# A scan over a matrix product: w loaded by row set over all partitions, other first cuts of x, and a shorter float32 warm-up of TensorE

## The chip, the cores and the metric

The kernel runs on one core of one Trainium2 chip. The metric is the device time of one execution in microseconds; the table below gives the runs. The engines are TensorE (PE, with its weight loads PEld), VectorE (DVE), ScalarE (ACT), GpSimd (POOL) and SyncE (SP); transfers are issued by SP, ACT and POOL and done by 16 DMA engines.

## The reference

```python
def setup_inputs():
    B, S, D = (16, 2048, 1024)
    return {'x': np.random.randn(B, S, D).astype(np.float32),
            'w': np.random.randn(D, D).astype(np.float32),
            'decay': (0.9 * np.random.rand(D) + 0.05).astype(np.float32)}

def reference(x, w, decay):
    xw = x @ w
    out[:, 0, :] = xw[:, 0, :].copy()
    for t in range(1, S):
        out[:, t, :] = decay[None, :] * out[:, t - 1, :] + xw[:, t, :]
```

A product of 32,768 rows with a 1024 x 1024 matrix, and then along the time axis of each batch a decayed running sum, with one decay for each column.

## The kernel before, in words

**Tiles.** The 16 x 2048 time steps are cut into 64 chunks of 512 (`TL`); two neighbouring chunks make a group. A group's product is made in eight slots of 128 output columns (`n`), each from eight sets of 128 rows of w (`k`): 4,096 products of 128 x 128 with 128 x 512 in bfloat16. The result stands with columns on partitions and time along the free axis, so VectorE can scan along time (`tensor_tensor_scan`, L229 and L210), transposes it back in 32 x 32 blocks (L266) into the `ot` buffers, and SP stores it.

**x.** A chunk is loaded by POOL in four DMAs, one for each quarter `q` of the 1024 columns of x; quarter `q` lands on partitions 32q to 32q+31, cast from float32 to bfloat16 on the way (`load`, L105). VectorE transposes 32 x 32 blocks of pairs of bfloat16 numbers, seen as float32 (`turn`, L115), into `xw`, in which the numbers of even and odd rows of w alternate; ScalarE or VectorE copies them apart into `xt` (`part`, L123). Some products read `xw` directly (`pairs`). Row `2p+e` of set `m` in quarter `q` of w thus meets partition `32q+p`.

**w.** w comes in four pieces `(h, e)`: half `h` of the columns, `e` for even or odd rows. A piece has four sets `m`. `load_w` (L307) loads a piece in four DMAs, one for each quarter of the partitions; each brings all four sets for its 32 partitions. Piece (0, 0) comes in float32, two DMAs from SP and two from ACT; the other three come from POOL, cast to bfloat16 (`load_part`, deeds U0 to U2). `settle` (L314) copies one set of a piece to `wsb`, in the order of columns that the products want (deeds W on VectorE, w on ScalarE). The staging buffers are the `ot` buffers of the output, not yet in use.

**The opening.** The first two chunks are handled in two parts each, whose sizes stand in `cuts`, in blocks of 32 time steps: 9 and 7 of chunk 0, 8 and 8 of chunk 1. For each part: load (deeds M0 to M3), transposition by set (E), copy by set (G on ScalarE, F on VectorE). The products of the first four slots go part by part: first part of chunk 0, all even sets and then all odd sets, four slots each; its second part in the same way; then chunk 1's first part by pairs of sets, and its second part slot by slot.

**Warm-up.** Before any data is there, TensorE multiplies zeros (`spin`, L332): 22 products of the zeroed tile `idle`, 128 x 512 in bfloat16. Then come `gate` products: for each quarter of x's first part, ScalarE copies one number of it into a zeroed tile `gate` (`spin_on`, L348, deeds K0 to K3), and TensorE makes products with that tile, 3, 3, 3 and 1 of them; so they start when that quarter has landed.

**Order.** The order of each engine's instructions is written out by hand: `agenda` lists deeds by slot, -99 is the opening, and every instruction is kept in program order on its engine (`pin`). The POOL queue has eight semaphores for its DMAs in turn: the ninth load waits at its issue for the landing of the first, and so on. The deed L takes the next x load of the list `loads`.

Of the kernel before, what the change touches and what calls it, by code (L numbers as in the profile page):

```python
# [9 lines left out]
FP32 = mybir.dt.float32  # L10
BF16 = mybir.dt.bfloat16
# [3 lines left out]
def _ap(ap_obj: bass.AP, new_ap, extra_offset=0):  # L15
    return dataclasses.replace(
        ap_obj,
        ap=[list(p) for p in new_ap],
        offset=ap_obj.offset + extra_offset,
    )  # L20
# [5 lines left out]
def kernel(  # L26
# [26 lines left out]
    nc = tc.nc  # L53
    pin = tc.keep_in_program_order
    B, S, D = x.shape
    assert w.shape == (D, D)

    NQ = 4
    P = 32
    CQ = D // NQ  # L60
    K = CQ // P
    M = K // 2
    TL = 512
    NJ = TL // P
    NC = S // TL
    R = K // 2
    CH = D // 2
    CR = CH // NQ

    const = ctx.enter_context(tc.tile_pool(name="const", bufs=1))  # L70
# [5 lines left out]
    def ring(pool, name, count, shape, dtype=FP32):  # L76
        i = turns[name] = turns.get(name, -1) + 1
        return pool.tile(shape, dtype, name=f"{name}{i % count}")

    def quad(q):  # L80
        return slice(q * P, (q + 1) * P)
# [12 lines left out]
    def ot_tile(nj):  # L94
        return ring(sb, "ot", 4, [128, nj, CR])
# [3 lines left out]
    xt_of = {}  # L99
# [25 lines left out]
    def matmul(ps, n, k, xt, t0=0, t1=TL, start=0, pairs=None):  # L125
        if pairs is None:
            rhs = xt[:, k // 2, k % 2, t0:t1]
        else:
            rhs = pairs[:, k // 2, t0 // P:t1 // P, :, k % 2].rearrange("p j i -> p (j i)")
        lhs = wsb[:, k, n].rearrange("p q i -> p (q i)")  # L130
        pin(nc.tensor.matmul(  # L131
            out=ps[:, t0:t1] if ps.shape[1] >= t1 else ps,
            lhsT=lhs,
            rhs=rhs,
            start=(k == 0 and t0 == start),
            stop=(k == K - 1),
        ))
# [3 lines left out]
    class Tile:  # L141
# [45 lines left out]
        def copy(self):  # L187
            self.xs = sb.tile([128, 2 * TL], FP32, name=f"xs{self.lot % 3}")[:, 0:self.T]
            size = self.T // len(self.parts())
            for i, ps in enumerate(self.parts()):  # L190
                pin(nc.scalar.copy(out=self.xs[:, i * size:(i + 1) * size], in_=ps))  # L191
# [82 lines left out]
    class Outlet:  # L274
# [8 lines left out]
        def store(self, b, t0):  # L283
# [4 lines left out]
            for j in range(0, self.nj, nj):  # L288
# [8 lines left out]

    room = [ot_tile(2 * NJ).rearrange("p j c -> p (j c)") for _ in range(2)]
    size = M * CH
    stage = {(0, 0): room[0][:, 0:size],  # L300
             (0, 1): room[0][:, size:size * 3 // 2].bitcast(BF16),
             (1, 0): room[1][:, 0:size // 2].bitcast(BF16),
             (1, 1): room[1][:, size // 2:size].bitcast(BF16)}

    def load_w(queues, h, e):
        for i, q in enumerate((0, 2, 1, 3)):
            pin(queues[i % len(queues)].dma_start(  # L307
                out=stage[h, e][quad(q)].rearrange("p (m d) -> p m d", m=M),
                in_=_ap(w, [[2 * D, P], [2 * P * D, M], [1, CH]],
                        (q * CQ + e) * D + h * CH)))  # L310

    def settle(h, e, m, copy):
        src = stage[h, e][:, m * CH:(m + 1) * CH]
        pin(copy(out=wcols[:, 2 * m + e, h],  # L314
                 in_=src.rearrange("p (q r i) -> p q r i", q=NQ, r=R)))

    idle = const.tile([128, TL], BF16, name="idle")
    spare = ring(psp, "spare", 1, [128, TL])
    rows = const.tile([128, 2, P], FP32, name="rows")
    touch = const.tile([128, 1], BF16, name="touch")  # L320
    load_w((nc.sync, nc.scalar), 0, 0)
    pin(nc.vector.memset(idle, 0.0))  # L322
    pin(nc.vector.memset(rows, 0.0))
    pin(nc.scalar.copy(out=touch, in_=idle[:, 0:1]))

    gates = [const.tile([128, 128], BF16, name=f"gate{q}") for q in range(NQ)]
    for gate in gates:
        pin(nc.vector.memset(gate, 0.0))

    def spin(count, by):  # L330
        for _ in range(count):
            pin(nc.tensor.matmul(out=spare, lhsT=by, rhs=idle, start=True, stop=True))  # L332

    spin(22, idle[:, 0:128])
    H = NJ // 2
    cuts = (((0, H + 1), (H + 1, NJ)), ((0, H), (H, NJ)))
    for q in range(NQ):
        pin(nc.sync.dma_start(
            out=rows[q * P:q * P + R],
            in_=_ap(decay, [[P, R], [CH, 2], [1, P]], q * CR)))  # L340
# [5 lines left out]

    def spin_on(q):
        pin(nc.scalar.copy(out=gates[q][quad(q), 0:1], in_=xb_of[0][quad(q), 0, 0:1]))  # L348
        spin(3 if q < NQ - 1 else 1, gates[q])

    def load_part(i):
        load_w((nc.gpsimd,), *((0, 1), (1, 0), (1, 1))[i])

    def part_one(i, copy):
        part(i // 8, copy, i % 4, i % 4 + 1, *cuts[i // 8][i // 4 % 2])
# [65 lines left out]
    def turn_and_load(c):  # L421
# [38 lines left out]
        "L": lambda i: load(*loads.pop(0)) if loads else None,  # L460
    }
    agenda = {
        -99: "M0 U0 M1 M2 M3 U1 U2 w0 W1 w2 W3 K0 K1 K2 K3 E0 E1 G0 E2 G1 E3 F2 G3 W4 w5 W6 W7 D E4 E5 G4 E6 G5 E7 F6 G7 E8 E9 G8 E10 G9 E11 F10 G11 E12 L E13 G12 L E14 G13 E15 L F14 G15",
        0: "p0 z0 W8 W9 W10 W11",
        1: "g0",
        2: "L S1 L",
# [89 lines left out]
    for step, (g, n) in enumerate(slots):  # L556
        T = TL * len(g)
        left = step - len(slots)
        if n % R == 0:
            ns, nj = range(n, n + R), T // P  # L560
            if left == -2 * R:
                outlets = [Outlet(ns, H, half) for half in range(2)]
            else:
                pieces = 1 if left < -7 * R else 2 if left < -6 * R else nj // H
                outlets = [Outlet(ns, nj, pieces=pieces)]
        if left == -R:
            outlets = []
        if step == 0:
            heads = [ring(psp, "ps", 3, [128, T]) for _ in range(3)]
            firsts = [ps[:, 0:TL] for ps in heads] + [spares[0]]  # L570
            seconds = [ps[:, TL:T] for ps in heads] + [spares[1]]
            for j0, j1 in cuts[0]:
                for e in range(2):
                    for k in range(e, K, 2):
                        for i in range(R):
                            matmul(firsts[i], i, k, xt_of[0], j0 * P, j1 * P, j0 * P,
                                   pairs=None if e else xw_of[0])
            for k0 in range(0, K, 2):
                for i in range(R):
                    for k in (k0, k0 + 1):  # L580
                        matmul(seconds[i], i, k, xt_of[1], 0, H * P,
                               pairs=xw_of[1] if k0 < 4 else None)
            for i in range(R):
                for k in range(K):
                    matmul(seconds[i], i, k, xt_of[1], H * P, TL, H * P,
                           pairs=xw_of[1] if i < 2 else None)
        if step < R:
            ps = heads[n] if n < 3 else tuple(spares)
        else:
            if step == K + 1:  # L590
                ps = nexts
            elif len(g) == 2 or n % R < 3:
                ps = ring(psp, "ps", 3, [128, T])
            else:
                ps = ring(psp, "spare", 1, [128, TL])
            todo = [(k, l) for k in range(K) for l in range(len(g))]
            if step < K:
                todo.sort(key=lambda kl: kl[0] % 2)
            elif step == K:
                todo = []  # L600
                nexts = (ring(psp, "spare", 1, [128, TL]), ring(psp, "ps", 3, [128, T])[:, TL:T])
                for l in range(len(g)):
                    for i, one in enumerate((ps[:, l * TL:(l + 1) * TL], nexts[l])):
                        for k in range(K):
                            matmul(one, n + i, k, xt_of.get(g[l]),
                                   pairs=xw_of[g[l]] if l or not i and k >= M else None)
            elif step == K + 1:
                todo = []
            if left == -1:
                ps = tuple(both[:, t:t + TL // 2] for t, both in zip(  # L610
                    (0, TL // 2), (ps, ring(psp, "ps", 3, [128, TL]))))
                blocks += [bank("spare1", 1), bank("ps", 3)]
                for t, half in zip((0, TL // 2), ps):
                    for k in range(K):
                        matmul(half, n, k, xt_of[g[0]], t, t + TL // 2, t)
                    if not t:
                        cross((1,), (0, 1))
                todo = []
            for k, l in todo:
                matmul(ps[:, l * TL:(l + 1) * TL], n, k, xt_of[g[l]])  # L620
        tiles.append(Tile(g, n, ps, outlets))
        do = agenda.get(step, agenda.get(left) if left >= -20 else None)
        if do is None:
            do = usual(step)
        else:
            do = do.split()
            if left == -20:
                do = rest(step) + do
        perform(do)
# [29 lines left out]
```

## Time and profile before

| what | value |
|---|---|
| median of 3 runs | 904.37 us (904.36 to 904.57) |
| profiled execution, its own time | 905.1 us |
| its span | 903.3 us |
| TensorE busy | 896.9 us (99%) |
| VectorE, ScalarE, GpSimd busy | 824.2, 685.9, 657.1 us |
| DMA moved | 204.77 MB, mean 227 GB/s |
| granted TensorE clock, mean | 1.000 |

The profile is of one execution; its times count from the start of the span. A row of the timeline gives start, duration, engine, line, operation, written tile <- read tiles, shapes and count, and in brackets how long the engine had been idle and what ended that. Stretches ("windows") give the busy time of each engine within them, then the granted clock, the DMA engines' share and GB/s. A load by POOL with a cast is counted with the bytes that it writes. A DMA's semaphore is raised in steps as its shares land; the trace holds the time of each step, and a landing is the last of them.

### The profile page before, as it was taken

Reading aid. Unit: us, or ns where it says so; the run is one execution under the profiler, and the core shown is the slowest. Engines: PE = TensorE matmul, PEld = TensorE weight load, DVE = VectorE, ACT = ScalarE, POOL = GpSimd, SP = SyncE. Lnnn points to the kernel's source line nnn. Section 1 sums busy time; section 2 is a strip of 40 time slices with the busy share of each in tenths; the row PEclk is TensorE's granted clock in tenths of the full one; section 3 lists DMA queues with packets and bytes.
Section 4 is the critical chain, followed back from the end, with each engine's and each line's share of the span. In section 5 each row is a group of like instructions: output and inputs, shape, how many; then the busy total and the mean of one; then the engine's idle time right before and its main releaser. Section 6 shows DMA issues by size and latency. Waiting matters only on the chain.

```text
span 903.3 us, 12163 instructions
## 1 busy us (share of the span) xinstructions
PE 896.9 (99%) x4216; PEld 412.8 (46%) x4216; DVE 824.2 (91%) x632; ACT 685.9 (76%) x957; POOL 657.1 (73%) x755
## 2 busy tenths in 40 slices
PE   9999999999999999999999999999999999999998
PEld 5444444444444444444444444444444444444444
DVE  4899998998999999999998999999999999999998
ACT  4899867877877877878778778777787787787743
POOL 7978678877767778777677687777777776876632
PEclk9999999999999999999999999999999999999999
DMA  9999999999999999999999999999999999999858
GB/s 193 184 215 215 223 244 208 215 229 232 248 239 251 253 241 246 250 258 249 241 237 226 222 231 226 232 229 227 233 227 226 233 231 222 227 230 214 184 143 232
DMA packets 403182, 204.77 MB, mean 227 GB/s; under 512 B 9392, under 2 KB 402096, under 8 KB 403120
## 3 DMA queue, kind: packets, MB, share of 16 engines
q1 hardware_dynamic: 265808, 134.77, 60.9%
q0 software_dynamic: 137024, 68.70, 56.4%
q8 instruction: 33, 0.54, 0.2%
q10 hardware_dynamic: 288, 0.52, 0.2%
q14 instruction: 29, 0.24, 0.1%
HBM read 138.42 MB, written 134.22 MB: 302 GB/s over the span
## 4 chain that ended last, share of the span: by engine, by line
PE 92%; DMA 3%; DVE 2%; issue 1%; POOL 1%; ACT 0%; DVEq 0%; POOLq 0%; ACTq 0%
PE ps L131 91%; DMA xb<-in_x_dram 2%; POOL xb L105 1%; DMA ot<-in_w_dram 1%; PE spare L131 1%; DVE so L229 1%; DVE ot L266 0%; DVE so L210 0%; DVE xw L115 0%; POOL xs L205 0%; PE spare L392 0%; PE ps L392 0%; ACT h L171 0%; DVE h L401 0%; POOL so L199 0%
## 5 line engine op out<-in xcount | busy, mean ns | idle before, releaser
L131 PE MATMUL ps<-xt,wsb 128*128 128x512 bf16 (+1 forms) x4024 | 865.6, 378 | 0.4 <-DVE so L229 0.4
L131 PEld LDWEIGHTS <-wsb 128*128 128x128 bf16 x4168 | 407.3, 98 | 479.0 <-issue 1.7
L205 POOL TENSOR_TENSOR xs<-h,xs 128x512 f32<-128x512 f32 (+1 forms) x190 | 242.8, 1278 | 183.1 <-ACT h L171 84.6
L266 DVE STREAM_TRANSPOSE ot<-so 128x1024 f32<-128x1024 f32 (+2 forms) x264 | 300.1, 1175 | 5.7 <-DMA out_dram<-ot 3.6
L191 ACT COPY xs<-ps 128x1024 f32<-128x1024 f32 (+1 forms) x190 | 188.8, 994 | 145.2 <-PE ps L131 141.6
L254 POOL TENSOR_TENSOR so<-h,xs 128x512 f32<-128x512 f32 (+1 forms) x190 | 241.1, 1271 | 48.0 <-ACT h L171 28.1
L123 ACT COPY xt<-xw 128x2048 bf16<-128x2048 bf16 (+3 forms) x136 | 242.1, 1788 | 8.9 <-DVE xw L115 8.9
L105 POOL DMA_DIRECT2D xb<-in_x_dram x264 | 174.2, 661 | 6.7 <-DMA xb<-in_x_dram 3.1
L171 ACT ACTIVATE h<-so,dec 128x512 f32<-128x512 f32 (+1 forms) x190 | 145.3, 765 | 37.3 <-DVE so L210 34.0
L115 DVE STREAM_TRANSPOSE xw<-xb 128x2048 f32<-128x2048 f32 (+3 forms) x78 | 147.4, 1902 | 8.8 <-DMA xb<-in_x_dram 8.8
L210 DVE TENSOR_TENSOR_SCAN so<-spare,keep,xs 128x512 f32<-128x512 f32 (+1 forms) x97 | 119.6, 1236 | 24.1 <-POOL xs L205 23.9
L210 DVE TENSOR_TENSOR_SCAN so<-spare,xs 128x512 f32<-128x512 f32 x93 | 113.2, 1219 | 26.4 <-POOL xs L205 23.5
L171 ACT ACTIVATE h<-ps,dec 128x512 f32<-128x512 f32 (+1 forms) x190 | 129.9, 683 | 0.0
L229 DVE TENSOR_TENSOR_SCAN so<-dec,ps 128x1024 f32<-128x1024 f32 x34 | 76.8, 2261 | 1.0 <-ACT h L171 1.0
L229 DVE TENSOR_TENSOR_SCAN so<-dec,keep,ps 128x1024 f32<-128x1024 f32 (+1 forms) x35 | 75.9, 2169 | 0.0
L258 ACT COPY keep<-so 128x1 f32<-128x1 f32 x136 | 25.3, 189 | 9.6 <-DVE so L229 9.0
L201 ACT COPY so<-keep 128x1 f32<-128x1 f32 x97 | 18.4, 191 | 2.7 <-DVE ot L266 2.5
L131 PE MATMUL ps<-xw,wsb 128*128 128x256 bf16 (+3 forms) x72 | 12.3, 306 | 0.4 <-DVE xw L115 0.4
L131 PE MATMUL spare<-xt,wsb 128*128 128x512 bf16 (+3 forms) x60 | 12.6, 330 | 0.0
L199 POOL MEMSET so<- 128x1 f32 x93 | 10.6, 116 | 0.6 <-DVE ot L266 0.6
L332 PE MATMUL spare<-idle 128*128 128x512 bf16 x22 | 7.4, 515 | 1.2 <-DVE idle L322 1.2
L307 POOL DMA_DIRECT2D ot<-in_w_dram x12 | 6.5, 545 | 1.0 <-issue 0.4
(39 smaller groups left out, 37.9 us busy)
## 6 DMA issues: line engine op xcount, KB each, us to landing
out_dram<-ot SPq DMA_DIRECT2D x236, 512.0 KB, 11.1
xb<-in_x_dram POOLq DMA_DIRECT2D x248, 256.0 KB, 7.9
out_dram<-ot SPq DMA_DIRECT2D x56, 128.0 KB, 2.6
out_dram<-ot SPq DMA_DIRECT2D x8, 256.0 KB, 4.0
ot<-in_w_dram POOLq DMA_DIRECT2D x12, 128.0 KB, 6.1
xb<-in_x_dram POOLq DMA_DIRECT2D x8, 128.0 KB, 4.8
out_dram<-xb SPq DMA_DIRECT2D x3, 256.0 KB
xb<-in_x_dram POOLq DMA_DIRECT2D x4, 144.0 KB, 6.2
```

The lines of the kernel that those rows point to most:

```text
L105: pin(nc.gpsimd.dma_start(out=xb_of[c][quad(q), j0:j1], in_=_ap(x, [[D, P], [P * D, j1 - j0], [1, CQ]], (b * S + t0 + j0 * P) * D + q * CQ)))
L115: pin(nc.vector.transpose(out=dst.rearrange("p (m j i) -> p j m i", m=M, i=P)[:, j0:j1, m0:m1], in_=src.rearrange("p (j m c) -> p j m c", ...
L123: pin(copy(out=xt_of[c][:, m0:m1, :, j0 * P:j1 * P], in_=src))
L131: pin(nc.tensor.matmul(out=ps[:, t0:t1] if ps.shape[1] >= t1 else ps, lhsT=lhs, rhs=rhs, start=(k == 0 and t0 == start), stop=(k == K - 1),))
L171: pin(nc.scalar.activation(out=h[:, i * size:(i + 1) * size], in_=src, func=mybir.ActivationFunctionType.Copy, scale=dec[:, self.n:self.n ...
L191: pin(nc.scalar.copy(out=self.xs[:, i * size:(i + 1) * size], in_=ps))
L205: pin(nc.gpsimd.tensor_tensor(out=odds, in0=self.g, in1=odds, op=ALU.add))
L210: pin(nc.vector.tensor_tensor_scan(out=so[:, 3:T + 2:2], data0=squares[-1][:, n:n + 1].to_broadcast([128, T // 2]), data1=self.xs[:, 1:T:2 ...
L229: pin(nc.vector.tensor_tensor_scan(out=so[:, t + 2:t + 2 + size], data0=dec[:, n:n + 1].to_broadcast([128, size]), data1=ps, initial=befor ...
L254: pin(nc.gpsimd.tensor_tensor(out=self.so[:, 2:T + 2:2], in0=self.h, in1=self.xs[:, 0:T:2], op=ALU.add))
L258: pin(nc.scalar.copy(out=self.keep, in_=self.so[:, self.T + 1:self.T + 2]))
L266: pin(nc.vector.transpose(out=outlet.ot[:, :, c0:c0 + P], in_=self.so[:, 2 + t0:2 + t0 + nj * P].rearrange("p (i t) -> p i t", t=P)))
```

## The change

Four things change together, all in the opening; the agenda of the slots behind it is the same.

- `load_w` loads one set `m` of a piece for all 128 partitions in one DMA, instead of all four sets for 32 partitions. The source of such a DMA is written as 4 quarters x 32 rows x 512 columns, the destination as 128 partitions x 512. Of piece (0, 0), set 0 comes from SP and set 1 from ACT in float32; sets 2 and 3 come from POOL, cast to bfloat16 (the new U0), and POOL issues them ahead of x's first part. The other three pieces become U1 to U3, at the places where U0 to U2 were.
- The first parts of chunks 0 and 1 become 10 and 7 blocks of 32 time steps, instead of 9 and 8.
- The warm-up is four products of a zeroed float32 tile `wide` (128 x 512) with its own first 128 columns, instead of 22 in bfloat16. `idle` becomes a view of half of `wide`.
- Each gate makes one product, instead of 3, 3, 3 and 1.

```diff
-    stage = {(0, 0): room[0][:, 0:size],
-             (0, 1): room[0][:, size:size * 3 // 2].bitcast(BF16),
+    stage = {(0, 1): room[0][:, size:size * 3 // 2].bitcast(BF16),
              (1, 0): room[1][:, 0:size // 2].bitcast(BF16),
              (1, 1): room[1][:, size // 2:size].bitcast(BF16)}
 
-    def load_w(queues, h, e):
-        for i, q in enumerate((0, 2, 1, 3)):
-            pin(queues[i % len(queues)].dma_start(
-                out=stage[h, e][quad(q)].rearrange("p (m d) -> p m d", m=M),
-                in_=_ap(w, [[2 * D, P], [2 * P * D, M], [1, CH]],
-                        (q * CQ + e) * D + h * CH)))
+    def spot(h, e, m):
+        if (h, e) == (0, 0):
+            if m < 2:
+                return room[0][:, m * CH:(m + 1) * CH]
+            return room[0][:, 2 * CH:3 * CH].bitcast(BF16)[:, (m - 2) * CH:(m - 1) * CH]
+        return stage[h, e][:, m * CH:(m + 1) * CH]
+
+    def load_w(queue, h, e, m):
+        pin(queue.dma_start(
+            out=spot(h, e, m),
+            in_=_ap(w, [[CQ * D, NQ], [2 * D, P], [1, CH]],
+                    (2 * P * m + e) * D + h * CH)))
 
     def settle(h, e, m, copy):
-        src = stage[h, e][:, m * CH:(m + 1) * CH]
         pin(copy(out=wcols[:, 2 * m + e, h],
-                 in_=src.rearrange("p (q r i) -> p q r i", q=NQ, r=R)))
-
-    idle = const.tile([128, TL], BF16, name="idle")
+                 in_=spot(h, e, m).rearrange("p (q r i) -> p q r i", q=NQ, r=R)))
+
+    wide = const.tile([128, TL], FP32, name="wide")
+    idle = wide[:, 0:TL // 2].bitcast(BF16)
...
-    load_w((nc.sync, nc.scalar), 0, 0)
-    pin(nc.vector.memset(idle, 0.0))
+    load_w(nc.sync, 0, 0, 0)
+    load_w(nc.scalar, 0, 0, 1)
+    pin(nc.vector.memset(wide, 0.0))
...
-    def spin(count, by):
+    def spin(count, by, on):
         for _ in range(count):
-            pin(nc.tensor.matmul(out=spare, lhsT=by, rhs=idle, start=True, stop=True))
-
-    spin(22, idle[:, 0:128])
+            pin(nc.tensor.matmul(out=spare, lhsT=by, rhs=on, start=True, stop=True))
+
+    spin(4, wide[:, 0:128], wide)
     H = NJ // 2
-    cuts = (((0, H + 1), (H + 1, NJ)), ((0, H), (H, NJ)))
+    cuts = (((0, H + 2), (H + 2, NJ)), ((0, H - 1), (H - 1, NJ)))
...
-        spin(3 if q < NQ - 1 else 1, gates[q])
+        spin(1, gates[q], idle)
 
     def load_part(i):
-        load_w((nc.gpsimd,), *((0, 1), (1, 0), (1, 1))[i])
+        for m in range(0 if i else 2, M):
+            load_w(nc.gpsimd, i // 2, i % 2, m)
...
-        -99: "M0 U0 M1 M2 M3 U1 U2 w0 W1 ...
+        -99: "U0 M0 U1 M1 M2 M3 U2 U3 w0 W1 ...
...
+            Q = cuts[1][0][1] * P
             for k0 in range(0, K, 2):
                 for i in range(R):
                     for k in (k0, k0 + 1):
-                        matmul(seconds[i], i, k, xt_of[1], 0, H * P,
+                        matmul(seconds[i], i, k, xt_of[1], 0, Q,
                                pairs=xw_of[1] if k0 < 4 else None)
             for i in range(R):
                 for k in range(K):
-                    matmul(seconds[i], i, k, xt_of[1], H * P, TL, H * P,
+                    matmul(seconds[i], i, k, xt_of[1], Q, TL, Q,
                            pairs=xw_of[1] if i < 2 else None)
```

## The prediction

> **What bounds the kernel now.** I read the page first, then the chain that ended last in order of time, then the timeline of the opening, then the stretches of one microsecond from 2 to 7 us. The page and its chain by line:
>
> ```profile
> PE 896.9 (99%) x4216; PEld 412.8 (46%) x4216; DVE 824.2 (91%) x632; ACT 685.9 (76%) x957; POOL 657.1 (73%) x755
> ...
> PE ps L131 91%; DMA xb<-in_x_dram 2%; POOL xb L105 1%; DMA ot<-in_w_dram 1%; PE spare L131 1%; DVE so L229 1%; DVE ot L266 0%; DVE so L210 0%; DVE xw L115 0%; POOL xs L205 0%; PE spare L392 0%; PE ps L392 0%; ACT h L171 0%; DVE h L401 0%; POOL so L199 0%
> ```
>
> TensorE is the bound, and the change leaves its real work alone. So the end moves only if the unbroken run of products begins earlier or later. The chain in order of time shows where that run begins and what stands before it:
>
> ```profile
> 1.31 6.19 DMA xb<-in_x_dram
> ...
> 15.70 6.52 DMA ot<-in_w_dram
> ...
> 28.51 11.19 DMA xb<-in_x_dram
> ...
> 65.62 2.32 DVE so L229
> 67.98 806.51 PE ps L131 x3736
> ```
>
> Up to 39.7 us the chain is transfers, from there to 67.98 VectorE, then only TensorE. The opening, in the timeline:
>
> ```profile
> 6.29 1.83 PEld L332 LDWEIGHTS <-idle 128*128 128x128 bf16 x9 [0.27 <-issue]
> ...
> 9.77 1.56 DVE L115 STREAM_TRANSPOSE xw<-xb 128x288 f32<-128x288 f32 x4 [2.05 <-DMA xb<-in_x_dram]
> ...
> 10.61 0.55 PE L131 MATMUL ps<-xw,wsb 128*128 128x288 bf16 x3
> ...
> 15.31 0.46 PE L131 MATMUL ps<-xw,wsb 128*128 128x224 bf16 x3 [0.38 <-DVE xw L115]
> ...
> 39.83 2.31 DVE L115 STREAM_TRANSPOSE xw<-xb 128x2048 f32<-128x2048 f32 x1 [1.38 <-DMA xb<-in_x_dram]
> ```
>
> The first transposition waits for x's first part, whose last quarter landed at 9.64 (last completion event of its DMA). It ended at 10.25, yet the first real product starts at 10.61: ten gate products were still running, 0.3 us lost. After that TensorE's step from start to start exceeds columns / 2.4 GHz in three places that matter: 0.16 us at 12.52 (w of odd rows), 0.54 at 14.65 (second part of x), 0.61 at 67.15 (VectorE's L229). What the transfers do meanwhile, by windows (last columns: clock, DMA share, GB/s):
>
> ```profile
> 3.00:4.00 1.00, 1.00 (x4) 0.33 (x3) 0.00 (x0) 0.16 (x1) 1.00 (x3) 1.00 1.03 340
> 4.00:5.00 1.00, 1.00 (x3) 0.30 (x2) 0.00 (x0) 0.00 (x0) 1.00 (x3) 1.00 1.01 279
> 5.00:6.00 1.00, 1.00 (x4) 0.43 (x3) 0.00 (x0) 0.00 (x0) 1.00 (x2) 1.00 1.26 230
> 6.00:7.00 1.00, 1.00 (x6) 0.37 (x5) 0.05 (x1) 0.08 (x1) 0.01 (x1) 1.00 1.35 173
> ```
>
> The engines are full from 3 us on: float32 w by SP and ACT first, then POOL's casting loads (GB/s there counts written bytes, half of what is read). POOL's first packet leaves at 5.22, as the SP and ACT packets run out.
>
> **The change, part by part.** The sum is made against the profiled execution: 905.1 us, of which 903.3 are span and 1.8 lie around it; the median of the runs is 0.73 lower.
>
> *Fewer warm-up products.* 22+10 become 4+4. The gates' backlog goes, -0.3 us. The memset of `wide` has twice the elements of `idle` (0.27 us), so warming starts 0.3 later, ahead of nothing. Fewer DMAs on ACT (one, 0.45 us) and SP (one, 0.4 us) only bring forward the table load and the decay loads, for which nobody waits before 12.6.
>
> *Two w loads ahead of x on POOL.* Issuing costs 2 x 0.54 = 1.1 us, covered: POOL issued seven DMAs before its first packet left. The cover ends if packets could leave from 3.3 on (the load issued at 22.50 had packets 1.98 later), and still the queue is fed faster than it drains. The bytes are not covered: w loads of POOL land 0.65 us apart, so x stands 1.3 us further back; x's quarters grow from 288 to 320 rows of 1 KB. The x DMAs of 256 rows land 0.68 apart, so 320 take 0.85, four 3.4 us. SP and ACT move half as much: -256 KB each.
>
> *w by row set.* Here lies the main term. Each w DMA had 32 rows as its leading count, on both sides; now the source is led by 4 (`[CQ*D, NQ]`) and the destination by 128 partitions. The completion events say over how many of the 16 DMA engines a DMA is spread: every w DMA of before, led by 32, raises its semaphore in 16 arrivals; each decay DMA on SP, led by 4, in one at its issue (2.15 to 3.20) and four later, the last at 6.54, 7.35, 7.64 and 7.93. So a leading 4 gave four engines, and tiny transfers that end one after the other look like the same four for all. A source of 4 with a destination of 128 is not in the trace: bounds are four engines and sixteen. I take four, since a list of four entries cannot be handed out in more shares unless it is rewritten, and keep sixteen as a rival. The Trainium skill has a rule for it (DMA: Bandwidth & Descriptors, section on why a DMA increments its semaphore by 16): the largest number up to 16 that divides the leading sizes of both sides, and from SP and ACT the lowest-numbered engines. By it the answer is four, the same four for both DMAs; the decay rows agree, and no run shown has the mixed shape.
>
> Price on those engines: a 2 KB packet of SP or ACT took 84 ns (median, 2 to 4 us). 2 x 128 packets over four engines are 64 each, 64 x 0.084 = 5.4 us. On the same engines lie their shares of POOL's two w loads (1.3 us if POOL still spreads over 16; bounds 0 and 2.7, if it takes four engines too and those are other ones or the same) and of x (3.4). Sum 5.4+1.3+3.4 = 10.1 from about 1.9, so 12.0; last packet to landing took 0.73 (8.91 to 9.64): x lands at 12.7 (bounds 11.4 and 14.1; if SP's and ACT's DMAs take different fours, 2.7 us fall away: 10.0), 3.1 later. Then 0.13 to the transposition, 0.48 x 10/9 = 0.53 for it, 0.06 to the product: 13.4 for 10.61, +2.8.
>
> *Other cuts.* The first part gives 32 products of 320 columns, 32 x 0.136 = 4.3 us instead of 3.9; the x behind it has 192 rows a quarter, four times 0.5. So the 0.54 wait shrinks to about 0.2. w's odd rows come by set, the first set three DMAs (2.0 us) ahead of the last: the 0.16 goes. The last part, 288 columns, has four transpositions of about 0.4 to catch up with its first products: +0.2, where before all four had ended 0.3 us ahead (21.70 for 22.00). Sum -0.3. TensorE is then 2.5 late.
>
> *What is late next.* At 67.98 TensorE had lost 0.61 to VectorE, so its own lateness counts 1.9 there. VectorE's run up to it started at 39.83 after 1.38 of waiting for chunk 3 of x. Its inputs come from TensorE: 2.5-1.38 = 1.1 at least. Chunk 3 lands behind the same four engines, 3.1 late less 0.3 for the 64 rows a quarter moved forward: 2.8. If other engines were behind anyway (from first to last arrival that landing took 2.4 us, x's first one 0.6), less. I take 2.8, the last of the three; +1.9 to +4.2 by the bounds.
>
> Profiled 905.1+2.8 = 907.9; less 0.73, the median is **907.2**.
>
> **The rivals.**
> *Sixteen engines, not slower.* For it: the destination led by 128. SP and ACT then finish by 3.6 (512 KB at 389 GB/s), half the old time, and POOL's packets start between there and 5.22. x lands 1.3+3.4+0.7 later, 9.0 to 10.6; chunk 3 moves by that less 0.3, -1.0 to +0.6, TensorE by -1.2 to +0.4, of which VectorE lets no more than 1.0 show. Time 903.4 to 905.0, likeliest 904.1. It decides as soon as each w DMA's semaphore shows 16 arrivals.
> *The clock falls back.* The products stepped 0.427 us until 6.29 and 0.216 after: 5.1 us of work to full speed. The float32 transposes at the end step 0.109 for 128 columns, twice what bf16 takes there; at that factor four cold products last 3.4 us, at four times 6.8. Too short, or with a pause behind them, the real ones start at half clock: at most 5.1 us at half speed, +2.5, less the 0.6 at 67.15. On sixteen engines that gives 906.0. Against it: after the last product at 898.9 the granted clock stays 1.00 to the span's end, 4.4 us, and the pause on sixteen engines is 3.7 at most. The Trainium skill (TensorE: Matmul & The Clock Gate, section on the clock gate) lets it fall after one idle window of 3.4 us; the 4.4 us without a fall speak for a longer one. On four engines the gates open late and the pause passes 4.4: it can then add up to 2.5 to my forecast.
> *The warm-up doesn't warm,* the same price from a cause of its own: then the step of the first real products is 0.267.
>
> **How the numbers follow.** A measurement of this kernel tells about 0.2%, 1.8 us, from no change. Four engines 0.58, with its own range 906.3 to 909.5 (+1.9 to +4.2, and something for the clock above; two different fours, about as sixteen, are left to that case); sixteen 0.36; clock or warm-up alone 0.06, half of it over 1.8. Slower: 0.58 less 0.03 for its low end, plus 0.03 of the clock and 0.02 of sixteen: 0.60. Faster: it needs -1.8, beyond -1.0: 0.03. Same: 0.37. The range must reach into the sixteen-engine case to leave out no more than 2 in 10: 903.8 to 909.3.
>
> **What would show it.** Right: four arrivals late in the w DMAs of SP and ACT, packets of these two queues until 7 us or later, x's transposition near 13, the first 320-column product near 13.4, VectorE's wait before chunk 3 past 39.83. Wrong: 16 arrivals, SP and ACT quiet by 4, first product before 11. A step of 0.27 in the first products shows the clock. A wait elsewhere after 68 us would overturn the whole sum.

## The result, and the profile after

The changed kernel takes 916.89 us (median of 4 runs, 915.41 to 918.24), the kernel before 904.38 in the same job: ratio 1.0138, 95% interval 1.012 to 1.0155, so 12.5 us slower. The forecast was 907.2, with a range up to 909.3. The direction was right and the size was more than four times too small. The profiled execution took 915.41 us with a span of 913.6; it is the quickest of the four, so the profile holds 10.3 of the 12.5 us.

The page of the changed kernel: TensorE's busy time has hardly changed, and it still holds 90% of the chain, so the loss is a shift of the start and no slower work. The chain can be followed back only to 66.90 here, so it shows nothing of the transfers.

```profile
PE 898.5 (98%) x4196; PEld 412.1 (45%) x4196; DVE 826.6 (90%) x632; ACT 686.1 (75%) x957; POOL 659.7 (72%) x757
...
PE ps L131 90%; PE spare L131 1%; DVE so L229 0%; DVE ot L266 0%; DVE xw L115 0%; PE spare L399 0%; PE ps L399 0%; DVE h L408 0%; DVE so L210 0%; DVEq L115 0%
```

The chain of waits in order of time. The unbroken run of products has the same length to a hundredth, 806.51 us, and begins at 78.18 instead of 67.98, again right behind VectorE's L229:

```profile
75.82 2.32 DVE so L229
...
78.18 806.51 PE ps L131 x3736
```

The opening in the timeline (start, duration, engine, line, and in brackets the idle time before and what ended it):

```profile
1.46 6.44 PE L338 MATMUL spare<-wide 128*128 128x512 f32 x8 [1.46 <-DVE wide L328]
...
14.19 1.41 POOL L312 DMA_DIRECT2D ot<-in_w_dram  x2 [7.61 <-DMA ot<-in_w_dram]
...
16.76 1.69 DVE L115 STREAM_TRANSPOSE xw<-xb 128x320 f32<-128x320 f32 x4 [2.07 <-DMA xb<-in_x_dram]
...
17.36 1.01 PE L131 MATMUL ps<-xw,wsb 128*128 128x320 bf16 x3
...
29.78 1.56 DVE L115 STREAM_TRANSPOSE xw<-xb 128x288 f32<-128x288 f32 x4 [2.38 <-DMA xb<-in_x_dram]
...
33.78 2.27 DVE L229 TENSOR_TENSOR_SCAN so<-dec,ps 128x1024 f32<-128x1024 f32 x1
...
49.17 2.31 DVE L115 STREAM_TRANSPOSE xw<-xb 128x2048 f32<-128x2048 f32 x1 [0.15 <-DMA xb<-in_x_dram]
```

Three things are to be seen. x's first part is transposed at 16.76 instead of 9.77, and the first product follows at 17.36 instead of 10.61 (+6.75). POOL stands still for 7.61 us until 14.19: its ninth load waits for the semaphore of the first, a w load. And chunk 3 is transposed at 49.17 instead of 39.83 (+9.34), so 2.4 us more was lost behind x's first part, which was 6.99 late. VectorE waited only 0.15 us for chunk 3 itself, for 1.38 before. It was late already: its first scan starts at 33.78, behind the last part of x and the copies of U2's four sets, which landed at 32.12 to 33.52. In the timeline of the kernel before, that scan stands 9.04 earlier:

```profile
24.74 2.27 DVE L229 TENSOR_TENSOR_SCAN so<-dec,ps 128x1024 f32<-128x1024 f32 x1
```

The stretches of the changed kernel, with the clock, the DMA engines' share and GB/s in the last columns:

```profile
3.00:4.00 1.00, 1.00 (x2) 0.34 (x1) 0.00 (x0) 0.39 (x2) 1.00 (x2) 1.00 0.40 77
...
5.00:6.00 1.00, 1.00 (x3) 0.45 (x2) 0.00 (x0) 0.00 (x0) 1.00 (x3) 1.00 0.57 141
...
15.00:16.00 1.00, 0.99 (x2) 0.21 (x2) 0.00 (x0) 0.28 (x2) 1.00 (x2) 0.50 0.54 42
```

From 3 to 7 us the engines moved 77 to 141 GB/s where the kernel before moved 173 to 340. At 15 they moved 42, since POOL had issued nothing for 7.6 us. The clock is at half from 10.42 to 20.66. Its first record in the trace is at 7.00; the 1.00 of the rows before that stands for no record, and the float32 products step 0.854 us there and 0.427 with the clock up (in after_warm).

The completion events say which transfers were narrow. ACT's w DMA has one arrival at 2.12 and four at 6.65 to 6.96; SP's one at 2.09 and four at 11.76 to 12.30. POOL's first w load (set 2) has twelve arrivals at 3.49 to 3.75 and four at 13.45 to 13.91; its second (set 3) eight at 4.08 to 4.35, four at 7.61 to 9.02 and four at 14.03 to 14.37. x's quarters had twelve arrivals by 9.79, 11.63, 12.66 and 13.87; their last four came at 14.68, 15.00, 15.83 and 16.64. That fits one set of four engines that held everything up, and x landed at 16.64 instead of 9.64.

### The profile page after: what moved, and what is told of

It reads as the page before. It is cut to its first block, busy times and chain, and to the rows that moved or that the text cites. A ratio compares the mean times of both kernels' runs of the same rounds, so it can differ in the third digit from the quotient of the medians.

```text
span 913.6 us, 12110 instructions
## 1 busy us (share of the span) xinstructions
PE 898.5 (98%) x4196; PEld 412.1 (45%) x4196; DVE 826.6 (90%) x632; ACT 686.1 (75%) x957; POOL 659.7 (72%) x757
## 4 chain that ended last, share of the span: by engine, by line
PE 91%; DVE 1%; issue 0%; DVEq 0%
PE ps L131 90%; PE spare L131 1%; DVE so L229 0%; DVE ot L266 0%; DVE xw L115 0%; PE spare L399 0%; PE ps L399 0%; DVE h L408 0%; DVE so L210 0%; DVEq L115 0%
## 5 line engine op out<-in xcount | busy, mean ns | idle before, releaser
L254 POOL TENSOR_TENSOR so<-h,xs 128x512 f32<-128x512 f32 (+1 forms) x190 | 241.2, 1271 | 44.2 <-ACT h L171 28.6
L123 ACT COPY xt<-xw 128x2048 bf16<-128x2048 bf16 (+4 forms) x136 | 242.3, 1790 | 10.7 <-DVE xw L115 10.7
L115 DVE STREAM_TRANSPOSE xw<-xb 128x2048 f32<-128x2048 f32 (+4 forms) x78 | 147.4, 1901 | 8.6 <-DMA xb<-in_x_dram 7.2
L229 DVE TENSOR_TENSOR_SCAN so<-dec,ps 128x1024 f32<-128x1024 f32 x34 | 76.9, 2262 | 0.7 <-ACT h L171 0.6
L229 DVE TENSOR_TENSOR_SCAN so<-dec,keep,ps 128x1024 f32<-128x1024 f32 (+1 forms) x35 | 75.9, 2169 | 0.0
L312 POOL DMA_DIRECT2D ot<-in_w_dram x14 | 9.7, 700 | 9.2 <-DMA ot<-in_w_dram 7.6
L131 PE MATMUL ps<-xw,wsb 128*128 128x512 bf16 (+4 forms) x72 | 14.0, 328 | 0.8 <-DVE xw L115 0.8
L131 PE MATMUL spare<-xt,wsb 128*128 128x512 bf16 (+5 forms) x60 | 12.6, 330 | 0.0
L318 DVE COPY wsb<-ot 128x512 bf16<-128x512 bf16 x8 | 2.6, 331 | 9.3 <-DMA ot<-in_w_dram 9.2
```

What stands on the lines that cost most here:

```text
L115: pin(nc.vector.transpose(out=dst.rearrange("p (m j i) -> p j m i", m=M, i=P)[:, j0:j1, m0:m1], in_=src.rearrange("p (j m c) -> p j m c", ...
L123: pin(copy(out=xt_of[c][:, m0:m1, :, j0 * P:j1 * P], in_=src))
L131: pin(nc.tensor.matmul(out=ps[:, t0:t1] if ps.shape[1] >= t1 else ps, lhsT=lhs, rhs=rhs, start=(k == 0 and t0 == start), stop=(k == K - 1),))
L229: pin(nc.vector.tensor_tensor_scan(out=so[:, t + 2:t + 2 + size], data0=dec[:, n:n + 1].to_broadcast([128, size]), data1=ps, initial=befor ...
L254: pin(nc.gpsimd.tensor_tensor(out=self.so[:, 2:T + 2:2], in0=self.h, in1=self.xs[:, 0:T:2], op=ALU.add))
```

## The experiments

Times are medians; every ratio is against runs of the kernel before in the same job (medians 904.38 to 904.64). "Chunk 3" is the start of its transposition (L115, 128 x 2048) in the profile; "x" is the landing of the last quarter of x's first part.

| kernel | time, us | ratio, 95% interval | x | chunk 3 | span |
|---|---|---|---|---|---|
| before | 904.5 | | 9.64 | 39.83 | 903.3 |
| before_warm | 904.91 | 0.9995 to 1.0013 | 9.59 | 37.58 | 902.6 |
| before_cuts | 904.40 | 0.9994 to 1.0012 | 9.92 | 38.78 | 902.4 |
| before_warm_cuts | 905.29 | 0.9997 to 1.0015 | 10.52 | 39.27 | 903.6 |
| w16_w | 905.88 | 1.0007 to 1.0025 | 10.89 | 39.85 | 904.3 |
| w16_x_first | 907.05 | 1.0017 to 1.0038 | 8.40 | 39.56 | 904.0 |
| w16_all | 906.84 | 1.0012 to 1.0034 | 11.90 | 40.89 | 905.5 |
| u0_four | 907.96 | 1.0023 to 1.005 | 12.23 | 41.45 | 906.5 |
| w16_sw | 910.27 | 1.0049 to 1.0077 | 14.37 | 43.71 | 908.4 |
| u123_four | 911.34 | 1.006 to 1.0091 | 11.33 | 45.68 | 910.1 |
| w16_hw | 912.98 | 1.0081 to 1.0108 | 13.71 | 45.51 | 910.0 |
| w_only | 915.73 | 1.0109 to 1.0137 | 15.95 | 48.65 | 913.3 |
| changed kernel | 916.89 | 1.012 to 1.0155 | 16.64 | 49.17 | 913.6 |
| after_warm | 917.58 | 1.0122 to 1.0153 | 17.03 | 51.51 | 916.7 |

Span less chunk 3 is 863.5 to 865.2 in every row: what has been lost by chunk 3 stays lost, to within 1.7 us.

**Which transfers must be wide.** The theory was that the four engines make the loss. Its rival was that order, cuts and warm-up do. In w16_all every w load is issued again in four DMAs, one for each quarter of the partitions, so with 32 rows leading on both sides; the bytes and the order of the pieces stay, but U0 is now four DMAs instead of two.

```diff
+    def load_q(queue, h, e, q, m0, m1):
+        ...
+        pin(queue.dma_start(
+            out=dst[quad(q)].rearrange("p (m d) -> p m d", m=m1 - m0),
+            in_=_ap(w, [[2 * D, P], [2 * P * D, m1 - m0], [1, CH]],
+                    (q * CQ + 2 * P * m0 + e) * D + h * CH)))
...
-    load_w(nc.sync, 0, 0, 0)
-    load_w(nc.scalar, 0, 0, 1)
+    for q in (0, 2, 1, 3):
+        load_q(nc.sync if q in (0, 1) else nc.scalar, 0, 0, q, 0, 2)
...
-        for m in range(0 if i else 2, M):
-            load_w(nc.gpsimd, i // 2, i % 2, m)
+        for q in (0, 2, 1, 3):
+            load_q(nc.gpsimd, i // 2, i % 2, q, 0 if i else 2, M)
```

> The changed kernel, but every w DMA is led by 32 rows on both sides again: of piece (0, 0), sets 0 and 1 by two DMAs each on SP and ACT, sets 2 and 3 by four on POOL ahead of x; the other pieces by four DMAs each. Bytes, order of the pieces, cuts and warm-up are those of the changed kernel. Theory A (a w DMA led by 4 runs on four engines, and x waits behind those): all w semaphores show 16 arrivals, x's first part lands at 9.0 to 10.6 instead of 16.6, time 903.4 to 905.0. Rival B (x is late because two w loads stand ahead of it on POOL, and its first part is larger): x stays late, 912 or more. Rival C (the warm-up is too short, and the clock is half when the first products come): x early, but the first products step 0.267, time 906 or more.

Measured 906.84: ten of the 12.5 us are gone, and the first piece's loads show 16 arrivals within 0.5 to 1 us each, but for two stragglers in one of them. The timeline of this kernel:

```profile
8.05 0.54 POOL L322 DMA_DIRECT2D ot<-in_w_dram  x1 [0.48 <-DMA ot<-in_w_dram]
...
12.59 0.58 PE L131 MATMUL ps<-xw,wsb 128*128 128x320 bf16 x3
...
27.25 2.27 DVE L229 TENSOR_TENSOR_SCAN so<-dec,ps 128x1024 f32<-128x1024 f32 x1
```

POOL's idle stretch of 7.61 us has become 0.48, the first product comes at 12.59 and VectorE's first scan at 27.25. The first three products take 0.58 us, so the clock is up. So rivals B and C fall. That x landed only at 11.90, and that the time is 1.8 us above theory A's 903.4 to 905.0, was not expected; more on that below. Next, half of the edit each, with `load_q`: w16_hw widens only SP's and ACT's loads (the second hunk), w16_sw only POOL's (the third).

> The changed kernel with only SP's and ACT's w DMAs led by 32 rows; POOL's stay led by 4. Theory A with POOL's w DMAs on four engines too: the shared four lose 64 packets of 84 ns, 5.4 us, and keep POOL's set 2 (32 packets, 2.7 us) and x (3.4 us): x lands near 11.2 instead of 16.6, time 909 to 911.5. If the four engines of SP and ACT were the whole cost: 904 to 905. Rival B: 912 or more.

> The changed kernel with only POOL's w DMAs led by 32 rows; SP's and ACT's stay led by 4. Theory A: the four engines carry 5.4 us of SP and ACT, 1.3 of POOL's w and 3.4 of x, as in the sum of the prediction: x lands at 12.7, time 907 to 909, up to 911 if the clock falls as well. If POOL's four-engine DMAs were the whole cost: 904 to 905. Rival B: 912 or more.

Measured 912.98 and 910.27. So POOL's narrow loads alone are worth 6.1 us over w16_all, more than was expected (x landed at 13.71 for 11.2). SP's and ACT's alone are worth 3.4, within the expectation only with the part that the clock was given; x landed at 14.37 for 12.7. Of w16_hw, 912.98 lies in the range given to rival B, but w16_all has the same order of the pieces and takes 906.84. In w16_sw SP's DMA lands at 11.74, hardly earlier than in the changed kernel (12.30). POOL's share was then parted: u0_four leaves only the two loads ahead of x by set, u123_four only the twelve behind it. The edit of u0_four against w16_all; in u123_four the first line reads `if i:`.

```diff
+        if i == 0:
+            for m in range(0 if i else 2, M):
+                load_w(nc.gpsimd, i // 2, i % 2, m)
+            return
         for q in (0, 2, 1, 3):
             load_q(nc.gpsimd, i // 2, i % 2, q, 0 if i else 2, M)
```

> As w16_all (every w DMA led by 32 on both sides, 906.84 us), but U0, the two w loads of POOL ahead of x, by row set as in the changed kernel, so on four engines; SP, ACT and U1 to U3 stay on sixteen. POOL's fourteen loads on four engines together were worth about 6 us (912.98 with SP and ACT wide, 906.84 with all wide). Theory D, the packets add up on those four engines, and what comes after the opening counts too: U0 makes 1 to 2.5 of the 6 us, by x's landing, 907.8 to 909.5. Theory E, all that counts is what stands ahead of x's first part: 912 to 913.

> The counterpart: as w16_all, but U1 to U3, the twelve w loads of POOL behind x's first part, by row set on four engines; U0, SP and ACT on sixteen. Theory D: the greater part of the 6 us, 910 to 912, with x's first part landing about as in w16_all (11.9 us), and chunk 3 late instead. Theory E (they have slack): 906.5 to 907.5.

Measured 907.96 (+1.1 over w16_all) and 911.34 (+4.5), as theory D had it. In u123_four x's first part and the first product (12.02) are no later than in w16_all, and the loss lies further on; its timeline and VectorE's rows:

```profile
12.02 0.59 PE L131 MATMUL ps<-xw,wsb 128*128 128x320 bf16 x3
...
26.10 1.56 DVE L115 STREAM_TRANSPOSE xw<-xb 128x288 f32<-128x288 f32 x4 [3.04 <-DMA xb<-in_x_dram]
...
30.23 2.28 DVE L229 TENSOR_TENSOR_SCAN so<-dec,ps 128x1024 f32<-128x1024 f32 x1
...
45.68 2.31 DVE L115 STREAM_TRANSPOSE xw<-xb 128x2048 f32<-128x2048 f32 x1 [0.36 <-DMA xb<-in_x_dram]
```

The last part of x, behind four of the narrow loads in POOL's queue, is transposed at 26.10 for 23.52 in w16_all; with the copies of U2's sets behind it, VectorE's first scan is 2.98 late, and chunk 3 4.79. For chunks 2 and 3 themselves VectorE waits only 0.31 and 0.36 us. By chunk 3's start the parts add up: 1.06 from before to w16_all, 0.56 for U0, 2.82 for SP and ACT (w16_sw), 4.79 for U1 to U3. The sum is 9.23, and the changed kernel has 9.34. That it fits so closely is in part luck, as each profile is one execution; by the medians, each over the kernel before in its own job, the same parts are 2.2, 1.3, 3.4 and 4.7, or 11.6 of the 12.5 us.

**The clock.** after_warm is the changed kernel with a longer warm-up, so that TensorE is not left idle.

```diff
     spin(4, wide[:, 0:128], wide)
+    spin(34, idle[:, 0:128], idle)
...
-        spin(1, gates[q], idle)
+        spin(3 if q < NQ - 1 else 1, gates[q], idle)
```

> The changed kernel with 34 products of bfloat16 zeros behind the four of float32, and 3, 3, 3 and 1 products at the gates, so that TensorE has work up to x's landing. Rival C's share: in the changed kernel the granted clock is 0.50 from 10.4 to 20.7 us and the first 16 products of 320 columns step 0.267 instead of 0.136, 2.1 us. If that counts in full: 2 us less, 914.5 to 915.3. If TensorE would have waited for later parts of x and w anyway: no change, 916 to 917.

Measured 917.58, with an interval that holds the changed kernel's ratio. The opening's products run at full clock there; the timeline's first three take 0.59 us for 1.01:

```profile
1.46 13.41 PE L338 MATMUL spare<-wide 128*128 128x512 f32 x42 [1.46 <-DVE wide L328]
...
17.72 0.59 PE L131 MATMUL ps<-xw,wsb 128*128 128x320 bf16 x3
...
23.56 1.16 DVE L115 STREAM_TRANSPOSE xw<-xb 128x192 f32<-128x192 f32 x4 [1.16 <-DMA xb<-in_x_dram]
```

So the clock at half speed is real in the changed kernel and cost nothing that shows: the next part of x came at 23.56 with the clock up, and at 23.43 with it down. The comparison is not quite clean, since in the profile of after_warm the clock falls later, from 40.40 to 43.81, and chunk 3 starts at 51.51. But its run with the highest mean clock, 0.999, took 915.74 us, within the changed kernel's 915.41 to 918.24 at 0.991 to 0.994.

**Warm-up and cuts alone,** on the kernel before; the edits are those of the change.

> The kernel before with the changed warm-up alone: four float32 products, and one product per gate. Left open so far: with every w DMA led by 32 the changed kernel still takes 906.84 us, 2.2 over the kernel before (904.64 in that job). Theory A, the order of w ahead of x on POOL makes those 2.2: then the warm-up alone costs nothing and takes away the backlog of the gates, first product 10.3 instead of 10.6, time 904.2 to 904.7. Theory B, the short warm-up makes them: the clock falls before the first product or rises late, up to 5 us at half clock, time 906 to 907.

> The kernel before with the first parts of chunks 0 and 1 cut at 10 and 7 blocks instead of 9 and 8, and nothing else. x's first part is 320 rows a quarter instead of 288. Theory A (order of w and x on POOL): the cuts cost 4 x 32 rows of x, about +0.35 us at the first product, and gain about as much at the second part, 904.4 to 905.0. Theory C, the cuts make the 2.2 us: 906 to 907.

> The kernel before with the changed warm-up and the changed cuts, w as before. Each alone was the same as before (904.9 and 904.4 for 904.5). But with w on sixteen engines and two of its sets by POOL ahead of x, the two together cost 1.0 (906.84 for 905.88). Theory F, the two together cost this in any case: 905.3 to 905.8. Theory G, they cost only where x is late already, since the first part then lands later by its 32 rows a quarter and nothing behind takes it up: 904.2 to 904.9, first product 10.5 to 10.7.

None differs from before by more than the measurement tells: 904.91, 904.40, 905.29. The last one settles nothing between its two theories, as its 905.29 lies at the edge of one and between both; x landed late in its profile (10.52), mostly because two of the last quarter's sixteen shares did. What the profiles of the first two do show is where small gains go. With the short warm-up the gates cause no backlog, in the timeline:

```profile
10.24 0.54 PE L131 MATMUL ps<-xw,wsb 128*128 128x288 bf16 x3
```

The first product is 0.37 earlier, and the wait for w's odd rows behind it has grown from 0.16 to 0.44. With the new cuts x lands 0.28 later and the first product starts at 10.61 as before, since the backlog of the gates had that much to spare. The waits of 0.16 and 0.54 are gone, and at 20.80 (last part) 0.52 us of new ones stand.

**w alone, narrow and wide.** w_only is the changed kernel with the old warm-up and cuts; w16_w is w16_all with them.

> The changed kernel with the warm-up and the cuts of the kernel before, so w by row set over all partitions alone, on four DMA engines. If the four engines and the order make nearly all of the +12.5 us: 915.5 to 917. If warm-up and cuts add something of their own on four engines (1 us or more): below 915.5.

> The changed kernel with all w DMAs led by 32 on both sides (as w16_all), and with the warm-up and the cuts of the kernel before: what is left of the change is that two sets of w's first piece come by POOL ahead of x, and the other pieces of w at their new places. Theory A (the order makes the 2.2 us): 906.0 to 907.0, x's last quarter at 11 to 12 us instead of 9.64. Theories B and C (warm-up or cuts): 904.4 to 905.0.

Measured 915.73 and 905.88. So the new w loading makes 11.2 of the 12.5 us, and 1.3 of them stay when all loads are wide. Warm-up and cuts make 1.2 and 1.0 on top, with overlapping intervals; whether they cost anything is not settled. The clock may have a part in it: four of w16_all's seven runs have a mean clock of 0.995 to 0.998 and took 906.48 to 907.68, the other three 905.62, 905.99 and 907.40, while w16_w's eleven runs all have 0.999 to 1.000. None of those four left a trace. One row of w_only warns against reading the first product as the end's measure:

```profile
14.57 4.39 PE L338 MATMUL spare<-wide,gate 128*128 128x512 bf16 x10 [6.40 <-ACT gate L354]
...
18.80 0.55 PE L131 MATMUL ps<-xw,wsb 128*128 128x288 bf16 x3
```

Ten gate products at half clock hold the first product until 18.80, 1.4 later than in the changed kernel, and the end comes no later: TensorE then waits less for what follows.

**The rest of 1.3 us: is it the order on POOL?** With all loads wide, x still lands at 10.89 in w16_w, 1.25 later than before, although half of SP's and ACT's bytes are gone. The experiment puts x's first part ahead of U0 again:

```diff
-        -99: "U0 M0 U1 M1 ...
+        -99: "M0 U0 U1 M1 ...
```

> As w16_w (all w DMAs on sixteen engines, old warm-up and cuts, 905.88 us; x's first part landed at 10.89 there), with the one difference that POOL issues x's first part ahead of U0, the two sets of w's first piece. Open: in w16_w the engines moved only about 90 to 140 GB/s between 5 and 9 us, where the kernel before moves 173 to 230. Theory H, U0's four DMAs ahead of x cost x their own 1.3 to 2.6 us and nothing more: x lands at 8.3 to 9.3, at before's pace of 0.65 to 0.75 us a quarter, and TensorE then waits for U0's sets instead, 904.5 to 905.9. Theory I, POOL's loads are slow in that stretch whatever their order, because they begin while SP's and ACT's run out: x's quarters land a good 1 us apart again, x at 9.6 to 11, 905.5 to 907.

x lands at 8.40, so for the landing theory H holds and theory I falls. Two stretches, first w16_w, then w16_x_first:

```profile
6.00:7.00 1.00, 1.00 (x7) 0.41 (x6) 0.00 (x0) 0.00 (x0) 1.00 (x2) 1.00 0.94 103
```

```profile
6.00:7.00 1.00, 1.00 (x5) 0.40 (x4) 0.00 (x0) 0.00 (x0) 0.86 (x3) 1.00 1.35 166
```

U0's two sets are 1.3 us of the queue, and x gains 2.5. Why POOL's loads run at 103 GB/s where w goes first stays open. The time, 907.05, did not follow H's 904.5 to 905.9, and lies at the upper end of I's 905.5 to 907. In the profile, ScalarE copies a set of U0, landed at 9.71, before it opens the gates, and the first product (12.75, for 11.55 in w16_w) waits behind ten gate products:

```profile
9.81 0.62 ACT L328 COPY wsb<-ot 128x512 bf16<-128x512 bf16 x1 [4.16 <-DMA ot<-in_w_dram]
...
10.58 2.33 PE L348 MATMUL spare<-wide,gate 128*128 128x512 bf16 x10 [1.74 <-ACT gate L364]
```

Its runs scatter from 905.77 to 908.21, and the profiled one is the quickest, with chunk 3 at 39.56. The four slowest (907.36 to 908.21) have a mean clock of 0.998 and the other four (up to 906.75) 1.000; whether that is cause or consequence isn't in a trace. So the rest of 1.3 us stays open: the order explains x's landing and not the time. No version tried beats the kernel before by more than the measurement tells.

## Why the prediction was wrong

*What bounds the kernel: right.* TensorE's unbroken run kept its 806.51 us; transfers, then VectorE, set its start.

*Four engines: right, and for more DMAs than it took.* SP's and ACT's w DMAs show four late arrivals, so the source's leading 4 decides over the destination's 128. The value taken for POOL, sixteen engines, was wrong: its loads have four late arrivals too. The forecast had that as a bound of 2.7 us for the two loads ahead of x. It had no term for the twelve behind.

The Trainium skill (DMA: Bandwidth & Descriptors, section on why a DMA increments its semaphore by 16) gives POOL's queue the same rule for the number of engines, but lets all sixteen post an arrival and takes the next four engines, in turn, for the next DMA. The trace agrees: POOL's first load has 12 and 4 arrivals, its second 8, 4 and 4, of which the last came 5 us after the middle four. That fits data on a free set of four, while the last four arrivals only stand in the line of the blocked engines; no row names an engine.

*x's landing: the term was mis-sized, 10.1 us for 14.0.* w16_sw is the case that the sum was made for, SP and ACT on four engines and POOL's w on sixteen: 12.7 was worked out and 14.37 measured, so the sum was 1.7 us short; some of this may be the unexplained slow stretch of w16_w and w16_all. POOL's first loads on four engines add 2.3 more (16.64), where the bound for it was 1.4 above the value taken. On the blocked engines SP's and ACT's 64 packets and the 32 of POOL's first load took from 1.9, the sum's own start, to 13.2 (its landing, 13.9, less 0.73), 11.3 us or 118 ns a packet. The row for 84 came from a stretch in which all sixteen engines drained two queues; it did not carry over to these four, on which three queues meet. Up to 14 us SP's packets took 96 ns (median) and POOL's of 1 KB 98; the rest of the 118 stays open.

*What is late next: the step that failed.* The prediction moved chunk 3 by x's lateness less 0.3, 2.8 us, and priced U1 to U3 at nothing. Chunk 3 moved by 9.34, and not by its own landing, for which VectorE waited 0.15 us: VectorE's first scan was already 9.04 late (33.78 for 24.74), since it must first transpose the last part of x and copy U2's sets. Of the 9.34, 4.79 come from U1 to U3 (u123_four, with x's first part no later than in w16_all): in the changed kernel six of the eight loads of U2 and U3 take 3.0 to 4.0 us from first to last arrival and the last lands at 37.2; in w16_all all eight take 1.5 to 1.7, and the last lands at 28.6. Nor did the sum hold the stop of POOL's queue, 7.61 us until 14.19: with eight semaphores in turn a late landing blocks the ninth load, and what stands behind it is issued late as well. The terms for the parts behind the first, -0.3 in sum, did not come true, probably for that reason: the wait of 0.54 for the second part was to shrink to 0.2, and measured 0.5 at 23.21; at 29.58 0.6 went on the last part, for which 0.2 was allowed.

*The small terms: right, and worth nothing.* The gates' backlog of 0.3 went (0.37 in before_warm) and was eaten by the next wait.

*The rivals.* Sixteen engines fell with the arrivals; its own price was low too: 904.1 was worked out for it, and w16_w and w16_all, which have it, measured 905.88 and 906.84. x behind two sets of w on POOL landed at 10.9 to 11.9 there and not at 9.0 to 10.6, but that is not the whole reason, since w16_x_first has x at 8.40 and 907.05. The clock did fall behind a warm-up with a long pause, but the price of up to 2.5 us on the end was wrong: after_warm keeps it up to 40.40 and gains nothing, as the next parts of x decide. The argument against a fall, 4.4 us of full clock at the end of the trace, was wrong as well. Here the clock was up from 7.00 to 10.42, 3.4 us with 0.9 us of products in them, and then fell. In the kernel before, the trace does record a fall, at 903.98, 0.7 us behind the span's end and 5.1 behind the last product. The Trainium skill (TensorE: Matmul & The Clock Gate, section on the clock gate) lets the clock fall after one idle window of 3.4 us. The trace agrees with that length, though the stretch up to 10.42 was not all idle.

*The range.* Its upper end, 909.3, was made from bounds for POOL's two loads ahead of x, with something for the clock. A bound for the other twelve, by an estimate 2.6 us each on four engines (four times the 0.65 between two landings on sixteen), would have taken in the result.

## What to carry to other kernels

Look at the leading count of both sides of a DMA, and check the arrivals of its semaphore: here 32 on both sides gave sixteen arrivals together, and a source led by 4 put 256 KB on four engines though the destination was led by 128. When an edit changes the form of a load, price every load that has the new form, behind the opening too, and ask what the queue's next free semaphore waits for. Judge a change in the opening by the first place from which nothing is recovered (here chunk 3's transposition, 863.5 to 865.2 us before the end in all profiles), not by the first product.

## What the runs showed of the hardware

- A product of 128 x 512 in float32 appears as two records of 0.854 us each at half clock, 1.71 together, four times the 0.427 of bfloat16.
- Each of POOL's narrow loads brought 384 packets of 4 bytes besides the sixteen of its arrivals: the trace of the changed kernel has 9824 of that size on POOL's queue for 278 DMAs, 14 of them such loads, and w16_all 4480 for 280, sixteen each. 384 is 12 x 32, which fits 32 on each of the twelve engines without data. Up to 5 us there are 660: 384 and 12 arrivals of the first load, 256 and 8 of the second.
- SP's and ACT's w DMAs, whose issue began together at 0.74, did not share their four engines evenly: ACT's first packet left at 2.18 and SP's at 4.09, and they landed at 6.96 and 12.30. A DMA of x over all engines was held up by the slowest four, by 2.8 us (13.87 to 16.64).
